# Group A's attention scores: one PSUM tile for each head instead of one for a pair of heads, and the sinks' exponentials in SBUF

## The chip, the cores and the metric

The kernel runs on one core of one Trainium2 chip. The metric is the device time of one execution in microseconds (us), from which the median over several runs is taken. The engines are named as in the profile: PE is the matrix engine (PEld is its loading of weights, which overlaps with matmuls), DVE is VectorE, ACT is ScalarE, POOL is GpSimd, and SP issues the DMAs. Each engine works through its own list of instructions in order and waits on semaphores for the others.

## The reference

One block of a streaming encoder on x of 1024 tokens by 1024 features: an input projection, two groups of attention heads side by side, an output projection with residual, and a feed-forward part. The change touches group A, eight heads that share two K/V heads, with a window of keys, a distance penalty and a learned sink for each head:

```python
n = rms_norm(h, norm1_g[layer])
proj = jnp.einsum('bsd,dp->bsp', n, w_in[layer])
qa, ka, va, qb, kb, vb = jnp.split(proj, split_at, axis=-1)
...
scores = jnp.einsum('bnqhgd,bnshd->bnhgqs', qc, kb).astype(jnp.float32) * (HEAD_DIM ** -0.5)
scores = scores - slopes[:, :, None, None] * dist
scores = jnp.where(valid[None, :, None, None, None, :], scores, NEG_INF)
m = jnp.maximum(jnp.max(scores, axis=-1, keepdims=True), sink)
p = jnp.exp(scores - m)
probs = (p / (jnp.sum(p, axis=-1, keepdims=True) + jnp.exp(sink - m))).astype(v.dtype)
out = jnp.einsum('bnhgqs,bnshd->bnqhd', probs, vb)
```

Group B is attention over nine chunks with a position bias and no sink. Both outputs are normalised and projected, and `h + squared-ReLU MLP` follows.

## The kernel before

Float32 operands are split into a high and a low part, so that one product takes two or three matmuls. The work runs in stages: the first projections, the attention of group A (about 42 to 184 us of the span), that of group B (to about 400 us), the output projection, and the two large feed-forward products.

Attention is cut into units. A `UnitA` is one pair of heads (`j`, 0 to 3; its two heads are `s` = 0 and 1) and two blocks of 128 query tokens (`i0` and `i0 + 1`; `b` = 0 and 1); there are 16. Tile names carry both, so `S_A0_4` holds the scores of pair 0 for blocks 4 and 5. The views shorten the names: `S_A0_4` stands in the order of instructions as `S_A_4` and a buffer number, in the trace as `S_A`. A unit has a first half, `score(0)` and `score(1)`, and a second half, two `turn`s and two `apply`s.

- `score(s)`: four matmuls write head `s`'s scores of both blocks into the PSUM tile `S` (line 129, called from `scores`). For each block DVE adds the bias and takes the row's negative maximum `nm` in one instruction (line 405, followed by a short read of the accumulator); ACT takes the exponentials and their sum `sm` (line 406). In `score(1)`, after both heads, ACT takes the two sinks' exponentials `es` (line 507, 128x2 each), DVE adds them to `sm` (line 508) and takes the reciprocal `rc` (line 509), and DVE and POOL scale the four blocks of probabilities `P` (line 512), two each.
- `turn(u)`: PE transposes blocks of `P` into the PSUM tile `pt` (line 132), ACT copies it to the high part of `T` (line 413) and DVE subtracts to get the low part (line 135).
- `apply(u)`: PE multiplies `T` with V into `av` (line 129); ACT copies one half of it to `yc` (line 548), DVE adds the other half into `Y` (line 549).

Before the change the tile `S` of a unit spans two PSUM banks: head 0's scores lie in the first, head 1's in the second, and `es` is written over the first four columns of head 0's. Two such tiles exist (`bufs=2`), and group B's tiles, of the same size, use the same two buffers:

```python
self.S = aps.tile([P, 2, 2, 2 * P], F32, tag="S", bufs=2, name=f"S_{self.name}")
...
es = self.S[:, 0, 0, :4]
```

PE's instructions keep the order in which the program is written (`pe` chains each matmul to the one before). While a unit's second half runs, the first half of the unit two further on is woven in (`interleave`, `look_ahead`, `LOOK_AHEAD = 2`), and `Filler` puts pieces of the next input projections between (`ip_qA`, `ip_kB` and so on; `A_FILL = 7` pieces for a unit). A projection ends with DVE scaling the accumulated bank into `ts_...` (lines 246 to 251), which frees the bank; the banks tagged `w` (three) are shared by projections and transposes. The order of instructions on DVE, ACT, POOL and SP is set by a scheduler when the kernel is built, from the data and buffer dependencies and its own estimates.

Of the kernel before, what the change touches and what calls it, by code (L numbers as in the profile page):

```python
# [8 lines left out]
F32 = mybir.dt.float32  # L9
# [6 lines left out]
P = 128  # L16
# [29 lines left out]
def kernel(  # L46
# [31 lines left out]
    small = ctx.enter_context(tc.tile_pool(name="small", bufs=4))  # L78
# [23 lines left out]
    nc.scalar.activation(warm, eps4, AF.Sqrt)  # L102


    small.tile([P, 120], F32, tag="pad", bufs=1, name="pad")

    last_load = [None]

# [19 lines left out]
    def matmul(*args, **kw):  # L128
        pe(nc.tensor.matmul(*args, **kw))  # L129
# [236 lines left out]
    aps = ap_.enter_context(tc.tile_pool(name="aps", bufs=1, space=PSUM, reuse_waits="tile"))  # L366
# [10 lines left out]
    def window(kind, i):  # L377

        nb = min(i, 1 if kind == "A" else 4) + 1
        return i - nb + 1, nb * P  # L380

    def scores(kind, i, Q, K, S):
        k0, n = window(kind, i)
        if n > 512:
            parts = [(S[:, 0, :320], 0, 320), (S[:, 1, :320], 320, 320)]
        else:
            w = max(n, 2 * P)
            parts = [(S[:, 0, :w], 0, w)]
        for hl in range(2):
            for dst, o, w in parts:  # L390
                matmul(
                    dst, Q[:, i * P : (i + 1) * P], K[hl][:, k0 * P + o : k0 * P + o + w],
                    start=hl == 0, stop=hl == 1,
                )

    def exponentials(kind, i, bias, init, S, pr, nm, sm):

        k0, n = window(kind, i)
        w = (2 if kind == "A" else 5) * P
        bs = bias[:, w - n : w]  # L400
        if n > 512:
            v = lambda a: a.rearrange("p (a b) -> p a b", a=2)
            nc.vector.tensor_tensor_reduce(v(pr[:, :n]), S[:, :, :320], v(bs), -1.0, init, ALU.add, ALU.min, nm)
        else:
            nc.vector.tensor_tensor_reduce(pr[:, :n], S[:, 0, :n], bs, -1.0, init, ALU.add, ALU.min, nm)  # L405
        nc.scalar.activation(pr[:, :n], pr[:, :n], AF.Exp, bias=nm, scale=-1.0, accum_out=sm)  # L406
        return k0, n, pr

    def stats(name):
        return [small.tile([P, 4], F32, tag=t, name=f"{t}_{name}") for t in ("nm", "sm", "rc")]  # L410
# [65 lines left out]
    class UnitA:  # L476
# [10 lines left out]
        def score(self, s):  # L487
            p, j = self.pair, self.pair.j
            if s == 0:
                self.nm, self.sm, self.rc = stats(self.name)  # L490
                self.S = aps.tile([P, 2, 2, 2 * P], F32, tag="S", bufs=2, name=f"S_{self.name}")
            pt = at.tile([P, 5 * P], F32, tag="P", bufs=6, name=f"P_{self.name}_{s}")
            h = 2 * j + s
            for b in range(2):
                scores("A", self.i0 + b, p.Q[s], p.K[j // 2 :: 2], self.S[:, s, b : b + 1])
            for b in range(2):
                c = slice(2 * s + b, 2 * s + b + 1)
                self.P[b, s] = exponentials(
                    "A", self.i0 + b, p.biases()[s], nsink[:, h : h + 1],
                    self.S[:, s, b : b + 1], pt[:, b * 2 * P : (b + 1) * 2 * P], self.nm[:, c], self.sm[:, c],  # L500
                )
            if s == 0:
                return
            es = self.S[:, 0, 0, :4]
            for s in range(2):
                c = slice(2 * s, 2 * s + 2)
                nc.scalar.activation(es[:, c], self.nm[:, c], AF.Exp, bias=psink[:, 2 * j + s : 2 * j + s + 1])
            nc.vector.tensor_tensor(self.sm, self.sm, es, ALU.add)
            nc.vector.reciprocal(self.rc, self.sm)
            for (b, s), (k0, n, q) in self.P.items():  # L510
                engine = nc.gpsimd if (b, s) in POOL_NORM else nc.vector
                engine.tensor_scalar(q[:, :n], q[:, :n], self.rc[:, 2 * s + b : 2 * s + b + 1], None, ALU.mult)
# [316 lines left out]
    X, F, S = {}, {}, {}  # L829
# [378 lines left out]
    g, p, n0 = order2[-GQ]  # L1208
    for q in (0, 2, 1, 3):
        for n in range(n0, n0 + GQ):  # L1210
            (uh, ul), (wh, wl) = ops2[n, p]
            c = slice(q * P, (q + 1) * P)
# [35 lines left out]
def build(arrays):  # L1248
    import concourse.bacc as _bacc

    nc = _bacc.Bacc("TRN2", target_bir_lowering=False, num_devices=1)
    args = [nc.dram_tensor(f"in_{n}_dram", arrays[n].shape, F32, kind="ExternalInput").ap() for n in _INS]
    args.append(nc.dram_tensor("out_0_dram", (SEQ, D), F32, kind="ExternalOutput").ap())
    with tile.TileContext(nc, schedule_with_timeline_sim=True) as tc:
        kernel(tc, *args)
    return nc
# [9 lines left out]
```

## Time and profile before

| what | value |
|---|---|
| median of 3 runs | 1073.88 us (1073.26 to 1074.16) |
| profiled execution, own time | 1074.59 us |
| its span, first to last instruction | 1072.5 us |
| mean granted TensorE clock | 0.996 |
| PE busy | 1050.7 us, 98% of the span |
| DVE, ACT, POOL busy | 706.3, 579.5, 416.7 us |

The spans of matmuls overlap: a matmul starts before the one ahead of it has ended, and its end is modelled, so a busy PE is not idle but need not be at its peak. What PE loses is read from its idle times and the granted clock. Some 22 us of the span are without a matmul, in the first projections, in group A's stage and at the very end.

### The profile page before, as it was taken

The numbers are of one execution on the slowest core, as the hardware profiler recorded it, in microseconds if no ns is written. First come the engines' busy times: TensorE is split into PE (matmuls) and PEld (weight loads), VectorE is DVE, ScalarE is ACT, GpSimd is POOL, SyncE is SP. The second block draws the span as 40 slices with busy tenths as digits, with TensorE's granted clock in tenths as the row PEclk, the third lists the DMA queues.
The fourth block names the chain that finished last, engine by engine and source line by source line (L and its number), as shares of the span: only waits on it lengthen the run. The fifth ranks groups of instructions, "written<-read, shape, count | busy, mean of one in ns | idle before, by whom it ended". The sixth has DMA issues, their size and how long they took to land.

```text
span 1072.5 us, 14369 instructions
## 1 busy us (share of the span) xinstructions
PE 1050.7 (98%) x5040; PEld 874.1 (82%) x5040; DVE 706.3 (66%) x1134; ACT 579.5 (54%) x994; POOL 416.7 (39%) x316
## 2 busy tenths in 40 slices
PE   7989999999999999999999999999999999999997
PEld 6877887888888888888888888888888888888885
DVE  4567778657667675696544434326889886778667
ACT  7666776656565465666544544554623333333346
POOL 1465766333361142405553464445015024024025
PEclk9999999999999999999999999999999999999999
DMA  9944626343457333133455344516998534532004
GB/s 328 261 114 115 171 89 173 101 111 112 134 191 282 129 108 137 79 98 118 181 172 177 140 135 158 190 65 235 317 403 302 182 126 161 178 119 96 1 1 157
DMA packets 90439, 170.17 MB, mean 159 GB/s; under 512 B 7808, under 2 KB 43520, under 8 KB 90368
## 3 DMA queue, kind: packets, MB, share of 16 engines
q1 hardware_dynamic: 90224, 169.25, 47.9%
q8 instruction: 40, 0.66, 0.2%
q14 instruction: 31, 0.25, 0.1%
q10 hardware_dynamic: 144, 0.00, 0.0%
HBM read 105.26 MB, written 45.09 MB: 140 GB/s over the span
## 4 chain that ended last, share of the span: by engine, by line
PE 86%; DVE 6%; issue 3%; DMA 2%; ACT 2%; SPq 1%; POOL 1%; DVEq 0%; ACTq 0%; POOLq 0%
PE f L129 27%; PE f_a L129 16%; PE f_c L129 8%; PE op_B L129 4%; PE f_b L129 4%; PE op_A L129 4%; PE ip_qB L129 4%; PE ip_kB L129 3%; PE ip_vB L129 3%; PE av_B L129 3%; PE pt_B L132 2%; PE S_B L129 2%; PE ip_qA L129 2%; PE S_A L129 1%; PE av_A L129 1%
## 5 line engine op out<-in xcount | busy, mean ns | idle before, releaser
L129 PE MATMUL f<-X,W 128*128 128x512 f32 x1344 | 305.9, 389 | 0.1
L129 PEld LDWEIGHTS f<-X,W 128*128 128x128 f32 x1344 | 252.0, 188 | 52.8 <-DVE X L135 0.5
L129 PE MATMUL f_a<-V,U 128*128 128x512 f32 x768 | 176.1, 389 | 0.0
L129 PEld LDWEIGHTS f_a<-V,U 128*128 128x128 f32 x768 | 144.1, 188 | 30.0
L135 POOL TENSOR_TENSOR U<-u,U 128x1024 fp32r<-128x1024 f32 x32 | 80.3, 2511 | 226.9 <-PE f_c L129 133.4
L135 POOL TENSOR_TENSOR W<-T,W 128x1024 fp32r<-128x1024 f32 x29 | 75.7, 2613 | 139.1 <-ACT W L934 139.1
L129 PE MATMUL f_c<-V,U 128*128 128x512 f32 x384 | 88.4, 389 | 0.0
L129 PEld LDWEIGHTS f_c<-V,U 128*128 128x128 f32 x384 | 72.1, 188 | 15.0
L934 ACT ACTIVATE V<-Z 128x1024 fp32r<-128x1024 f32 x32 | 33.9, 1060 | 90.6 <-PE f_a L129 44.6
L983 DVE TENSOR_TENSOR k<-f,k 128x1024 f32<-128x1024 f32 x24 | 29.3, 1221 | 61.9 <-PE f L129 61.9
L135 POOL TENSOR_TENSOR W<-w,W 128x1024 fp32r<-128x1024 f32 x23 | 57.3, 2492 | 32.2 <-ACT W L934 32.0
L934 ACT ACTIVATE V<-w 128x1024 fp32r<-128x1024 f32 x24 | 25.5, 1061 | 78.5 <-issue 34.2
L135 DVE TENSOR_TENSOR V<-w,V 128x1024 fp32r<-128x1024 f32 x24 | 47.2, 1972 | 27.4 <-ACT V L934 27.4
L934 ACT ACTIVATE U<-u 128x1024 fp32r<-128x1024 f32 x56 | 58.5, 1045 | 11.4 <-DMA ud<-k 7.8
L406 ACT ACTIVATE P_B<-P_B,nm_B 128x640 f32<-128x640 f32 (+2 forms) x64 | 44.4, 694 | 24.5 <-DVE nm_B L405 12.7
L977 ACT ACTIVATE k<-f 128x1024 f32<-128x1024 f32 x24 | 24.6, 1026 | 58.7 <-PE f L129 58.7
L129 PE MATMUL ip_kB<-nT,w_kB 128*128 128x512 f32 x192 | 51.5, 397 | 1.5 <-DVE T_A L135 0.8
L129 PE MATMUL op_A<-w_o,y 128*128 128x512 f32 x192 | 52.1, 397 | 0.5 <-DVE h L726 0.5
L129 PE MATMUL ip_vB<-nT,w_vB 128*128 128x512 f32 x192 | 51.9, 398 | 0.0
L934 ACT ACTIVATE W<-T 128x1024 fp32r<-128x1024 f32 x32 | 33.9, 1059 | 33.3 <-PE f L129 21.0
L129 PE MATMUL ip_qB<-nT,w_qB 128*128 128x512 f32 x192 | 51.5, 396 | 0.0
L129 PE MATMUL ip_qA<-nT,w_qA 128*128 128x512 f32 x192 | 51.3, 406 | 0.0
(212 smaller groups left out, 2033.2 us busy)
## 6 DMA issues: line engine op xcount, KB each, us to landing
w<-in_w_ff_dram SPq DMA_DIRECT2D x64, 512.0 KB, 4.7
u<-ud SPq DMA_DIRECT2D x56, 512.0 KB, 4.7
ud<-k SPq DMA_DIRECT2D x48, 512.0 KB, 3.2
KkB<-ts_kB SPq DMA_DIRECT2D x64, 128.0 KB, 2.3
yd<-y SPq DMA_DIRECT2D x14, 512.0 KB, 2.8
y<-yd SPq DMA_DIRECT2D x14, 512.0 KB, 7.1
xs<-in_xT_dram SPq DMA_DIRECT2D x16, 256.0 KB, 5.3
xr<-in_x_dram SPq DMA_DIRECT2D x8, 512.0 KB, 7.2
```

The source lines that it names most:

```text
L129: pe(nc.tensor.matmul(*args, **kw))
L132: pe(nc.tensor.transpose(*args))
L135: engine.tensor_tensor(lo, full, f(hi), ALU.subtract)
L406: nc.scalar.activation(pr[:, :n], pr[:, :n], AF.Exp, bias=nm, scale=-1.0, accum_out=sm)
L934: nc.scalar.activation(w[0], full, AF.Copy)
L977: nc.scalar.activation(kept[p], ps, AF.Copy)
L983: dve.tensor_tensor(v, ps, v, ALU.add)
```

## The change

Each head gets a PSUM tile `S` of its own, of the shape that group B uses, of which only the first bank is filled; still two buffers. The sinks' exponentials go to a small SBUF tile `es` with two buffers. A filler tile in the same SBUF pool is made smaller, so that later tiles keep their place.

```diff
-    small.tile([P, 120], F32, tag="pad", bufs=1, name="pad")
+    small.tile([P, 104], F32, tag="pad", bufs=1, name="pad")
...
             if s == 0:
                 self.nm, self.sm, self.rc = stats(self.name)
-                self.S = aps.tile([P, 2, 2, 2 * P], F32, tag="S", bufs=2, name=f"S_{self.name}")
+            S = aps.tile([P, 2, 512], F32, tag="S", bufs=2, name=f"S_{self.name}_{s}")
+            S = S[:, 0].rearrange("p (a b) -> p a b", a=2)
...
-                scores("A", self.i0 + b, p.Q[s], p.K[j // 2 :: 2], self.S[:, s, b : b + 1])
+                scores("A", self.i0 + b, p.Q[s], p.K[j // 2 :: 2], S[:, b : b + 1])
...
-                    self.S[:, s, b : b + 1], pt[:, b * 2 * P : (b + 1) * 2 * P], self.nm[:, c], self.sm[:, c],
+                    S[:, b : b + 1], pt[:, b * 2 * P : (b + 1) * 2 * P], self.nm[:, c], self.sm[:, c],
...
-            es = self.S[:, 0, 0, :4]
+            es = small.tile([P, 4], F32, tag="es", bufs=2, name=f"es_{self.name}")
```

PE's list has the same matmuls in the same order; its waits differ. The place shown is in the stretch near 57 us, where pair 0's unit of blocks 0 and 1 begins its `apply` (`av`) and head 1 of blocks 4 and 5 gets its scores (`S_A_4` before, `S_A_4_1` now). Before:

```order
L129 MATMUL av_A_0_723<-T_A_0_0_688,VA_175 128x256 [waits Activation_49]
L129 MATMUL av_A_0_723<-T_A_0_0_688,VA_175 128x256 [waits DVE_49]
L129 MATMUL S_A_4_707<-KA_171,QA_178 128x256 [waits DMAHW2_49,DMAHW0_49,DVE_49]
L129 MATMUL S_A_4_707<-KA_173,QA_178 128x256
L129 MATMUL S_A_4_707<-KA_171,QA_178 128x256
L129 MATMUL S_A_4_707<-KA_173,QA_178 128x256
```

Now:

```order
L129 MATMUL av_A_0_727<-T_A_0_0_692,VA_175 128x256 [waits Activation_49]
L129 MATMUL av_A_0_727<-T_A_0_0_692,VA_175 128x256 [waits DVE_49]
L129 MATMUL S_A_4_1_730<-KA_171,QA_178 128x256 [waits DMAHW2_49,DMAHW0_49]
L129 MATMUL S_A_4_1_730<-KA_173,QA_178 128x256
L129 MATMUL S_A_4_1_730<-KA_171,QA_178 128x256
L129 MATMUL S_A_4_1_730<-KA_173,QA_178 128x256
```

The wait for DVE ahead of head 1's scores is gone. It stands before each of the 16 units' head 1 before the change, and is left in one of them now (the first that takes a used buffer).

On DVE, the same place: the sinks' sum, reciprocal and scaling for blocks 2 and 3, the low part of the first transposes (`T_A_0_0`), and the maxima of blocks 4 and 5, head 0. Before:

```order
L508 TENSOR_TENSOR sm_A_2_629<-sm_A_2_629,S_A_2_631 128x4 [waits Activation_49]
L509 RECIPROCAL rc_A_2_630<-sm_A_2_629 128x4 [waits DVE_49]
L135 TENSOR_TENSOR T_A_0_0_688<-pt_A_0_0_687,T_A_0_0_688 128x256 [waits Activation_49]
L512 TENSOR_SCALAR P_A_2_0_632<-P_A_2_0_632,rc_A_2_630 128x256 [waits DVE_49]
L512 TENSOR_SCALAR P_A_2_1_661<-P_A_2_1_661,rc_A_2_630 128x256
L405 ISA P_A_4_0_708,nm_A_4_704<-S_A_4_707,b_A_318,nsink 128x256 [waits PE_49]
```

Now:

```order
L509 TENSOR_TENSOR sm_A_2_631<-sm_A_2_631,es_A_2_673 128x4 [waits Activation_49]
L510 RECIPROCAL rc_A_2_632<-sm_A_2_631 128x4 [waits DVE_49]
L513 TENSOR_SCALAR P_A_2_0_634<-P_A_2_0_634,rc_A_2_632 128x256 [waits DVE_49]
L513 TENSOR_SCALAR P_A_2_1_664<-P_A_2_1_664,rc_A_2_632 128x256
L135 TENSOR_TENSOR T_A_0_0_692<-pt_A_0_0_691,T_A_0_0_692 128x256 [waits Activation_49]
L405 ISA P_A_4_0_712,nm_A_4_708<-S_A_4_0_711,b_A_318,nsink 128x256 [waits PE_49]
```

`T_A_0_0`, for which `av` waits on PE, now stands behind the two scalings instead of ahead of them.

On ACT, the same place: the exponentials of head 1 of blocks 2 and 3, the two sinks' exponentials of that unit, and a weight copy of 128x1024 (`w_qA`). Before:

```order
L406 ACTIVATE P_A_2_0_632,sm_A_2_629<-P_A_2_0_632,nm_A_2_628 128x256 [waits DVE_49] x2
L252 ACTIVATE ts_qA_0_649<-ts_qA_0_649 128x512 [waits DMAHW4_49,DMAHW3_49,DMAHW5_49,DMAHW2_49,DMAHW6_49,DMAHW1_49,DMAHW7_49,DMAHW0_49,DVE_49]
L406 ACTIVATE P_A_2_1_661,sm_A_2_629<-P_A_2_1_661,nm_A_2_628 128x256 [waits DVE_49] x2
L507 ACTIVATE S_A_2_631<-nm_A_2_628,psink 128x2
L172 ACTIVATE w_qA_755<-st_qA_754 128x1024 [waits Pool_49]
L507 ACTIVATE S_A_2_631<-nm_A_2_628,psink 128x2 [waits Activation_49]
```

Now:

```order
L406 ACTIVATE P_A_2_0_634,sm_A_2_631<-P_A_2_0_634,nm_A_2_630 128x256 [waits DVE_49] x2
L508 ACTIVATE es_A_2_673<-nm_A_2_630,psink 128x2
L252 ACTIVATE ts_qA_0_651<-ts_qA_0_651 128x512 [waits DMAHW3_49,DMAHW4_49,DMAHW2_49,DMAHW5_49,DMAHW1_49,DMAHW6_49,DMAHW0_49,DMAHW7_49,DVE_49,Activation_49]
L406 ACTIVATE P_A_2_1_664,sm_A_2_631<-P_A_2_1_664,nm_A_2_630 128x256 [waits DVE_49] x2
L508 ACTIVATE es_A_2_673<-nm_A_2_630,psink 128x2
L172 ACTIVATE w_qA_761<-st_qA_760 128x1024 [waits Pool_49]
```

Head 0's sink now comes right behind head 0's exponentials, and head 1's stands ahead of the weight copy instead of behind it. The same is seen in the other units: the sinks come earlier on ACT, and on DVE the sum and the reciprocal stand ahead of the first addition into `Y` in 12 of them, as do POOL's two scalings ahead of its other work (`ts_...` and `w_...`) in several.

## Rows read from the trace of the kernel before

**Rows 1.** The page, part 1: busy us, share of the span, instructions.

```profile
PE 1050.7 (98%) x5040; PEld 874.1 (82%) x5040; DVE 706.3 (66%) x1134; ACT 579.5 (54%) x994; POOL 416.7 (39%) x316
```

**Rows 2.** Stretches: us, busy us (instructions) by engine, granted clock, DMA share, GB/s.

```profile
58.90:107.00 48.10, 44.95 (x238) 37.72 (x239) 34.32 (x99) 31.74 (x93) 27.82 (x30) 0.96 0.39 107
...
184.00:400.00 216.00, 214.34 (x1184) 181.37 (x1184) 149.19 (x376) 129.60 (x286) 80.35 (x95) 1.00 0.47 146
```

**Rows 3.** PE's and PEld's waits, 37 to 184 us: total, times, longest.

```profile
PE S_A L129 <- DVE nm_A L405: 3.3, 2, 1.9
PE pt_A L132 <- DVE ts_qA L249: 1.0, 1, 1.0
PE ip_kB L129 <- DVE T_A L135: 0.8, 1, 0.8
PE ip_kB L129 <- DVE ts_qA L249: 0.7, 1, 0.7
PE av_A L129 <- DVE T_A L135: 0.6, 1, 0.6
...
PEld S_A L129 <- DVE nm_A L405: 4.8, 5, 2.1
```

**Rows 4.** PE's timeline: start, us, instruction, [idle before and its releaser].

```profile
58.84 0.74 PE L129 MATMUL S_A<-KA,QA 128*128 128x256 f32 x4 [1.89 <-DVE nm_A L405]
...
77.30 0.75 PE L129 MATMUL S_A<-KA,QqA 128*128 128x256 f32 x4 [1.43 <-DVE nm_A L405]
...
90.77 0.66 PE L132 MATMUL pt_A<-ident,P_A 128*128 128x128 f32 x4 [1.03 <-DVE ts_qA L249]
...
99.93 1.67 PE L129 MATMUL ip_kB<-nT,w_kB 128*128 128x512 f32 x6 [0.68 <-DVE ts_qA L249]
```

**Rows 5.** DVE's timeline ahead of the first of these waits.

```profile
55.78 0.16 DVE L508 TENSOR_TENSOR sm_A<-sm_A,S_A 128x4 f32<-128x4 f32 x1 [2.17 <-ACT S_A L507]
...
56.43 1.55 DVE L512 TENSOR_SCALAR P_A<-P_A,rc_A 128x256 f32<-128x256 f32 x2
...
58.71 0.08 DVE L405 DVE_READ_ACCUMULATOR2_ANT nm_A<- 128x1 f32 x1
```

**Rows 6.** ACT's timeline at the same place.

```profile
54.55 1.04 ACT L172 ACTIVATE w_qA<-st_qA 128x1024 fp32r<-128x1024 f32 x1
...
55.50 0.25 ACT L507 ACTIVATE S_A<-nm_A,psink 128x2 f32<-128x2 f32 x1
```

**Rows 7.** Stretches around the first long wait, columns as in Rows 2.

```profile
57.00:58.80 1.80, 0.00 (x0) 0.00 (x0) 1.80 (x7) 0.38 (x1) 1.80 (x4) 1.00 0.22 48
...
60.40:63.70 3.30, 3.30 (x9) 2.60 (x8) 1.66 (x8) 2.46 (x9) 1.49 (x2) 0.50 0.57 159
...
63.80:75.90 12.10, 12.07 (x71) 10.25 (x69) 9.24 (x21) 7.22 (x19) 5.68 (x6) 1.00 0.32 75
```

**Rows 8.** Lines 507 and 144, small activations: ns min/median/max, first and last.

```profile
L507 ACT ACTIVATE S_A<-nm_A,psink x32: 242/248/267, 47.4 to 166.9; 128x2 f32<-128x2 f32 x32
...
L144 ACT ACTIVATE u_n<-ss,eps x10: 283/296/298, 22.4 to 455.0; 128x1 f32<-128x1 f32 x8, 128x4 f32<-128x4 f32 x2
```

**Rows 9.** DVE's and ACT's timeline ahead of the wait at 99.93 us.

```profile
97.45 0.42 DVE L549 TENSOR_TENSOR Y<-av_A,yc 64x256 f32<-64x256 f32 x1 [2.41 <-ACT yc L548]
...
99.20 0.68 DVE L249 SCALAR_TENSOR_TENSOR ts_qA<-ip_qA,R 128x512 f32<-128x512 f32 x1
...
95.24 1.06 ACT L172 ACTIVATE w_qB<-st_qB 128x1024 fp32r<-128x1024 f32 x1
```

**Rows 10.** DVE's and PE's timeline: a read ends, the same head's next scores.

```profile
44.17 0.09 DVE L405 DVE_READ_ACCUMULATOR2_ANT nm_A<- 128x1 f32 x1
...
47.52 0.72 PE L129 MATMUL S_A<-KA,QA 128*128 128x256 f32 x4
```

**Rows 11.** POOL's timeline: a weight's low part, then two scalings.

```profile
55.67 2.89 POOL L135 TENSOR_TENSOR w_qA<-st_qA,w_qA 128x256 fp32r<-128x256 f32 x4 [0.83 <-ACT w_qA L172]
58.54 1.82 POOL L512 TENSOR_SCALAR P_A<-P_A,rc_A 128x256 f32<-128x256 f32 x2
```


## The prediction

> **What bounds the kernel now.** I read the page first: PE is busy for 1050.7 us of a span of 1072.5 [rows 1], so the end moves only by what PE idles or runs slowly. Next the table of stretches. Group A's stage is the one with holes in the middle of the run: from 58.9 to 107 us PE is busy for 44.95 of 48.10 us at a granted clock of 0.96, while in group B, with DVE about as full, it is busy for 214.34 of 216.00 [rows 2]. Then the list of waits in that stage. The largest is "S_A waits for nm_A": head 1's scores wait for line 405 on DVE, 3.3 us as PE sees it (2 times), 4.8 us as the weight loads see it (5 times); the other four entries come to 3.1 us [rows 3]. The timeline puts the two long ones at 58.84 and 77.30 us [rows 4].
>
> What does this wait need? At 58.84 DVE has just read out the maximum of blocks 4 and 5 of head 0 (the read at 58.71 takes 0.08 us) [rows 5], and PE, which starts at once, writes head 1's scores of the same two blocks. They lie in another bank, and no number passes between the two. PE waits because both heads' scores are one tile. And DVE is late with that maximum since it stood still for 2.17 us for the sinks [rows 5]: on ACT the second sink came at 55.50, behind a weight copy of 1.04 us [rows 6].
>
> The clock tells of a second loss. PE is idle from 57.0 to 58.8. From 60.4 to 63.7 the granted clock is 0.50, that is 1.2 GHz in place of 2.4: PE is busy throughout, but starts 9 matmuls in 3.30 us, where the next stretch at 1.00 has 71 in 12.10 [rows 7]. That is the only fall from 58.9 to 107 us: 3.4 us at half speed out of 48.1 are what a mean of 0.96 leaves room for [rows 2]. The idle time of 1.43 us ahead of 77.30 [rows 4] brought none. So the first, longer one is the likely cause, and it is the wait that the change removes.
>
> **The change, part by part.**
>
> *The wait of head 1.* The list of PE loses it in 15 of 16 units. Price: 3.3 us by PE's idle times, 4.8 by those of the weight loads [rows 3]. Ends of matmuls are modelled and overlap with the next start, so PE's figure is too low by a little at each of the five waits, and the other is an upper end. I take 4.3.
>
> *The clock.* 3.4 us at half speed cost 1.7 us, and nothing if it falls all the same. I take 1.7, since the idle time before it should go almost wholly.
>
> *The sinks come earlier.* They no longer wait for head 1's part of the tile, so ACT takes head 0's sink right behind its exponentials, and the second one before the weight copy. In the unit of rows 5 and 6 that is 1.04 us earlier, and DVE's sum, reciprocal and scalings with it. At the wait at 99.93 us PE wants a bank that DVE frees by line 249 at 99.20 plus 0.68; ahead of that, DVE idled 2.41 us until an addition into Y, behind which the sum stood, and ACT spent 1.06 us on a weight copy amid the unit's exponentials [rows 9]. Now the copy comes after them and the sum before the addition, so the 0.68 us of waiting there [rows 4] should vanish. At 90.77 us (1.03 us [rows 4]) the same line 249 has moved ahead of one addition of 0.42 us and follows a sum that waits for one sink less (0.25 us): 0.7 of the 1.03 go. Of the wait of `ip_kB` for a transpose, 0.8 us [rows 3], I count 0.1. Bounds: nothing, and all three, 1.0 + 0.7 + 0.8 = 2.5 us. I take 1.5.
>
> *The sinks go to SBUF.* No row of before has this exponential with an SBUF target. The nearest is line 144, a small activation into SBUF of 296 ns against 248 for line 507 into PSUM [rows 8]: 0.05 us more, 32 times 1.6 us of ACT, which has room in group A (31.74 us busy of 48.10 [rows 2]). It touches the end only where DVE waits for the second sink: in every one of 16 units that would be 0.8 us, the upper bound; the lower is no difference. I take 0.1, two such places. The Trainium skill (ScalarE: Activation LUTs, Step-by-step: what each stage is for) speaks against the edit here: it says that ScalarE reaches PSUM faster than SBUF. The two rows agree in sign, though their functions differ (square root and exponential), and by either the sum moves by 0.8 us at most.
>
> *What is late next.* PE comes to its next waits some 2 to 4 us earlier. (a) `T_A_0_0` now stands behind two scalings, which took 1.55 us in the old place, with POOL at work beside them [rows 5]. DVE's sum can start about 1.0 us sooner, so `av` waits some 0.3 us longer than before; at worst 0.6 (1.55 less the 1.0). (b) POOL does its two scalings before the weight copy's low part, which began at 55.67 [rows 11]. The reciprocal is there at about 55.0, the two scalings take 1.82 us, a piece 2.89 / 4 = 0.72 [rows 11]: the first piece is ready at about 57.6. PE fell idle at 58.84 - 1.89 = 56.95; with 0.3 us of (a), the four scores (0.74) and five projection matmuls (1.67 / 6 = 0.28 each, ends overlapping) [rows 4] it needs the piece at about 59. Covered by a us or more; if scalings beside DVE's take longer, some 0.5 us. (c) DVE is busy for 34.32 of 48.10 us [rows 2], and the removed waits gave it time to catch up; it may end a transpose or a projection's scaling late in a few units. Bounds: nothing, and all that head 1 gave, 4.3 us. I take 0.8 of (c), which is one wait of the kind seen at 90 or 154 us, and 0.3 + 0.1 for (a) and (b).
>
> *Two buffers for single heads.* A head's scores now wait until the same head's tile of the unit before has been read. The smallest distance I find in the trace is at the beginning: the tile read at 44.17 plus 0.09, the same head's next scores at 47.52 [rows 10], so 3.3 us of room. Nothing is charged. After group A, PE has next to no waits [rows 2], so what is gained stays gained.
>
> **Sum**, against the profiled execution of 1074.59 us: 1074.6 - 4.3 - 1.7 - 1.5 + 0.1 + (0.3 + 0.1 + 0.8) = 1068.4. The median of the runs shown lies 0.7 us below the profiled one, so 1067.7.
>
> **The rivals.**
>
> 1. *The waits go, the clock falls or DVE takes part of it back.* DVE's late maxima were a sign that it was behind; PE would then stand at `av` (waiting for T) or at a bank in place of the scores. For it: the other four entries of the waits all name DVE [rows 3]. Against: DVE's idle times of 2.17 and 2.41 us show that it waits as well. If half of the 4.3 + 1.5 comes back and the clock falls, 1.7 + 2.9 less the 1.2 already counted: 1067.7 + 3.4 = 1071.1. The Trainium skill (TensorE: Matmul & The Clock Gate, A second HAM failure mode: psum-queue depth-cycling) describes a kernel in which small idle times between groups of matmuls were enough to make the clock swing. In this trace the 1.43 us ahead of 77.30 us were not enough [rows 4]; that counts against it.
>
> 2. *The change does nothing that can be measured.* Head 1's wait would be only the first of several on one chain through DVE (maximum, scaling, transpose's low part), and PE would wait as long a little later: 4.3, 1.7 and 1.5 all come back, and 1073.5 to 1073.9 remains. Against it: only 5 of the 16 units show that wait at all [rows 3], so DVE keeps up in general.
>
> 3. *Slower: the ring of two heads.* If DVE's reads of one unit fall more than 3.3 us behind, the next unit's scores of that head wait for them, where before a whole unit lay between. From 3.3 us of further lateness on, each us costs PE one us in each unit concerned. With 5 us of it, 1.7 more than the room, in four units: 4 x 1.7 = 6.8 us on top of the forecast, 1074.5, and with one more fall of the clock 1076.2. Against it: no such lateness is in the trace, and the sinks, which held DVE up ahead of 58.84 [rows 5], come earlier.
>
> **How the numbers follow.** The forecast gets 0.64, rival 1 0.20, rival 2 0.11, rival 3 0.05. About 0.2% (2.1 us) is what a measurement of this kernel can tell from no change, so the bound for "faster" is 1071.7. The forecast lies wholly on that side, of rival 1 most: 0.64 + 0.17 = 0.81 faster. Same: 0.03 + 0.11 + 0.01 = 0.15. Slower 0.04. The upper bounds of all gains with nothing given back make 1074.6 - 4.8 - 1.7 - 2.5 - 0.7 = 1064.9; a range of 1065.3 to 1071.9 leaves out the end of that, rivals 2 and 3.
>
> **What the profile after would show.** Right: no entry "S_A waits for nm_A" for PE, or one below 0.3 us; PE's granted clock at 1.00 from 58.9 to 107 us; in the stage of group A some 3 us less idle time for PE; the sum at line 509 without DVE idle times of 2 us ahead of it. Wrong: a new entry of more than 2 us for `av_A` waiting for T_A, or for the projections waiting for line 249; a clock of 0.50 somewhere in the stage; scores of either head waiting for nm_A of the unit before; or a first small-exponential duration far above 0.3 us. The prediction would also be wrong if the stage ended 6 us earlier and a later transfer of weights, started from it, held PE up in group B.

## The result, and the profile after

The changed kernel takes 1067.07 us, median of 6 runs (1066.10 to 1068.89). The kernel before, run beside it, takes 1073.91 us (6 runs, 1073.26 to 1075.31). The ratio on record is 0.9944, 95% interval 0.9933 to 0.9954; ratios here are not quotients of the two medians (that would be 0.9936), so the two differ a little throughout. Two more comparisons of the same pair, further below, gave 0.9951 and 0.9948. By these ratios the change gains 5.3 to 6.0 us; the medians of the three comparisons lie 6.8, 5.2 and 4.5 us apart. That is over twice the 0.2% that can be told from no change; the forecast was 1067.7.

The profiled execution took 1068.89 us, its span is 1067.0. Its page has these sums of busy time, to be held against [rows 1]:

```profile
PE 1049.3 (98%) x5040; PEld 874.3 (82%) x5040; DVE 710.5 (67%) x1134; ACT 578.5 (54%) x994; POOL 413.1 (39%) x316
```

No engine's work has changed by more than 4.2 us. The work is the same; what went is time in which PE stood idle or ran at half its clock. The waits of PE in group A's stage, from 37 to 184 us (engine, operation and line, what was waited for, us in total, times, longest), answer to [rows 3]:

```profile
PE av_A L129 <- DVE Y L550: 1.3, 1, 1.3
PE pt_A L132 <- DVE ts_vB L246: 0.6, 1, 0.6
PE av_A L129 <- DVE T_A L135: 0.6, 1, 0.6
PE ip_kB L129 <- DVE ts_qA L249: 0.4, 1, 0.4
PE ip_kB L129 <- DVE T_A L135: 0.2, 1, 0.2
```

"S_A waits for nm_A" is gone. The first two lines are new: one wait of 1.3 us for an addition into Y, and one of 0.6 us for a projection's bank. The timeline of PE, cut to the rows with a wait in brackets, shows where they stand (it answers to [rows 4]):

```profile
93.11 1.67 PE L129 MATMUL ip_kB<-nT,w_kB 128*128 128x512 f32 x6 [0.43 <-DVE ts_qA L249]
138.19 0.65 PE L132 MATMUL pt_A<-ident,P_A 128*128 128x128 f32 x4 [0.64 <-DVE ts_vB L246]
147.43 0.96 PE L129 MATMUL ip_kB<-nT,w_kB 128*128 128x512 f32 x3 [0.25 <-DVE T_A L135]
172.82 0.36 PE L129 MATMUL av_A<-T_A,VA 128*128 128x256 f32 x1 [1.29 <-DVE Y L550]
173.80 1.01 PE L129 MATMUL av_A<-T_A,VA 128*128 128x256 f32 x3 [0.62 <-DVE T_A L135]
```

From 58.9 to 92 us PE now does not wait at all. The table of stretches (length; busy us of each engine with the number of instructions that run in it, those across its edges included; PE's granted clock; share of the DMA engines; GB/s) says it again, beside [rows 2], and shows a second place:

```profile
58.90:107.00 48.10, 47.55 (x266) 40.26 (x265) 37.35 (x109) 34.10 (x99) 32.32 (x35) 1.00 0.48 135
168.00:184.00 16.00, 14.09 (x67) 11.53 (x66) 8.81 (x28) 8.11 (x20) 6.89 (x8) 0.89 0.53 149
184.00:400.00 216.00, 214.80 (x1188) 182.30 (x1187) 148.56 (x371) 129.82 (x285) 79.56 (x94) 1.00 0.48 151
173.70:177.10 3.40, 3.30 (x10) 2.92 (x11) 1.52 (x6) 0.08 (x1) 1.18 (x2) 0.52 0.41 103
```

From 58.9 to 107 us the clock is at 1.00 and 266 matmuls run where 238 did. But from 168 to 184 us, where group A ends and group B begins, it is 0.89: behind the two waits at 172.82 and 173.80 lie 3.4 us at about half clock, in which 10 matmuls run. Before the change this stretch ran at 1.00:

```profile
168.00:184.00 16.00, 15.38 (x82) 12.84 (x81) 13.69 (x37) 9.96 (x24) 9.40 (x12) 1.00 0.79 209
```

So the fall of the clock [rows 7] did not vanish, it moved. Because PE's matmuls keep their order, one and the same matmul can be found in both traces, and its start tells how much had been gained by then. Before, the end of group A reads:

```profile
178.85 0.34 PE L129 MATMUL av_A<-T_A,VA 128*128 128x256 f32 x1
179.81 0.62 PE L129 MATMUL av_A<-T_A,VA 128*128 128x256 f32 x3 [0.62 <-DVE T_A L135]
...
182.01 0.62 PE L129 MATMUL av_A<-T_A,VA 128*128 128x512 f32 x2
```

and after:

```profile
177.55 0.63 PE L129 MATMUL av_A<-T_A,VA 128*128 128x512 f32 x2
```

PE was ready for the first of these `av` at 172.82 - 1.29 = 171.53, against 178.85: 7.3 us gained by then. (The stage itself began 0.4 us later than before, its first scores at 42.46 against 42.09, so within the stage it is 7.7.) PE started that `av` 178.85 - 172.82 = 6.0 us earlier, and the last ones 182.01 - 177.55 = 4.5 us earlier: the new wait took 1.3 back and the halved clock some 1.5. At the end of the span it is 1072.5 - 1067.0 = 5.5 us. The 1 us more did not come bit by bit: it came in group B near 320 us, where PE before the change waits twice:

```profile
319.85 0.71 PE L129 MATMUL av_B<-padL,VvB 128*128 128x256 f32 x2 [0.23 <-ACT padL L413]
...
322.32 0.44 PE L132 MATMUL pt_B<-ident,P_B 128*128 128x128 f32 x2 [0.25 <-DVE VvB L135]
```

ACT's `padL` stands right behind its copy of an output weight (`w_o`, at 318.48), which had waited 2.56 us for a transfer. After the change the same copy waits 1.20 us, PE has no wait at these two matmuls, and its lead over the kernel before grows there from 4.4 us (317.84 against 313.40) to 5.6 (322.32 against 316.74). Why that transfer is waited for less is not followed here.

What is the new wait? It begins on the DMA queue. The rows that matter, from the timeline of all engines, in order of time:

```profile
162.34 0.52 SPq L439 DMA_DIRECT2D b_B<-in_relb_dram  x1
...
167.83 0.14 POOL L440 MEMSET b_B<- 64x64 f32 x1 [1.82 <-DMA b_B<-in_relb_dram]
168.03 0.15 POOL L441 MEMSET b_B<- 64x64 f32 x1
168.26 1.29 POOL L468 TENSOR_TENSOR sqA<-sqA,y 128x512 f32<-128x512 f32 x1
169.58 1.06 ACT L172 ACTIVATE w_vB<-st_vB 128x1024 fp32r<-128x1024 f32 x1 [2.21 <-POOL sqA L468]
170.55 0.71 ACT L406 ACTIVATE P_B<-P_B,nm_B 128x512 f32<-128x512 f32 x1
171.37 0.38 ACT L549 ACTIVATE yc<-av_A 64x256 f32<-64x256 f32 x1
172.26 0.42 DVE L550 TENSOR_TENSOR Y<-av_A,yc 64x256 f32<-64x256 f32 x1
```

A position bias of group B is issued at 162.34 and lands at 167.8, 5.5 us later. POOL stands still for it for 1.82 us, since it writes two masked corners into that tile (lines 440, 441). Its sum of squares `sqA` comes behind; ACT's weight copy waits 2.21 us for that sum; behind the copy stand an exponential and `yc`, behind `yc` DVE's addition into Y, and behind that PE's `av`. Before the change the same chain is in the trace, with a landing of 3.2 us and room to spare:

```profile
169.28 0.54 SPq L439 DMA_DIRECT2D b_B<-in_relb_dram  x1
...
172.47 0.14 POOL L440 MEMSET b_B<- 64x64 f32 x1 [2.62 <-DMA b_B<-in_relb_dram]
174.02 1.29 POOL L468 TENSOR_TENSOR sqA<-sqA,y 128x512 f32<-128x512 f32 x1
...
175.34 1.06 ACT L172 ACTIVATE w_vB<-st_vB 128x1024 fp32r<-128x1024 f32 x1 [0.49 <-POOL sqA L468]
```

The copy waited for 0.49 us there and PE not at all.

### The profile page after: what moved, and what is told of

It is laid out like the page before. It is cut to its first block, busy times and chain, and to the rows that moved or that the text cites. A ratio compares the mean times of both kernels' runs of the same rounds, so it can differ in the third digit from the quotient of the medians.

```text
span 1067.0 us, 14388 instructions
## 1 busy us (share of the span) xinstructions
PE 1049.3 (98%) x5040; PEld 874.3 (82%) x5040; DVE 710.5 (67%) x1134; ACT 578.5 (54%) x994; POOL 413.1 (39%) x316
## 4 chain that ended last, share of the span: by engine, by line
PE 91%; DVE 4%; DMA 2%; issue 1%; ACT 1%; SPq 1%; POOL 0%; DVEq 0%; ACTq 0%; POOLq 0%
PE f L129 27%; PE f_a L129 16%; PE f_c L129 8%; PE op_B L129 4%; PE f_b L129 4%; PE op_A L129 4%; PE ip_qB L129 4%; PE ip_kB L129 4%; PE ip_qA L129 4%; PE ip_vB L129 3%; PE av_B L129 3%; PE S_B L129 2%; PE pt_B L132 2%; PE S_A L129 1%; PE av_A L129 1%
## 5 line engine op out<-in xcount | busy, mean ns | idle before, releaser
L935 ACT ACTIVATE V<-w 128x1024 fp32r<-128x1024 f32 x24 | 25.4, 1060 | 81.1 <-issue 34.2
L135 DVE TENSOR_TENSOR V<-w,V 128x1024 fp32r<-128x1024 f32 x24 | 49.9, 2081 | 28.0 <-ACT V L935 27.1
L135 DVE TENSOR_TENSOR V<-Z,V 128x1024 fp32r<-128x1024 f32 x32 | 46.2, 1445 | 9.4 <-ACT V L935 5.9
```

The costliest lines, as they stand in the source:

```text
L135: engine.tensor_tensor(lo, full, f(hi), ALU.subtract)
L935: nc.scalar.activation(w[0], full, AF.Copy)
```

## The experiments

The theory: head 1's scores waited for head 0's maxima only because both lay in one tile; with two tiles that wait goes, and the earlier sinks, which is the second half of the change, shorten what is left on DVE. Rivals: the second half alone does it, since DVE's lateness came from the sinks; or SBUF as the place for the sinks brings the gain. Three comparisons were made, each with its own runs of the kernel before: there 1071.96 us in the first (17 runs, 1071.38 to 1074.32), 1073.03 in the second (15 runs, 1071.16 to 1074.86), 1072.85 in the third (10 runs, 1071.59 to 1075.12).

**The second half alone: shared tile, sinks in SBUF.** Against the kernel before:

```diff
-    small.tile([P, 120], F32, tag="pad", bufs=1, name="pad")
+    small.tile([P, 104], F32, tag="pad", bufs=1, name="pad")
...
-            es = self.S[:, 0, 0, :4]
+            es = small.tile([P, 4], F32, tag="es", bufs=2, name=f"es_{self.name}")
```

> One half alone: the sinks' exponentials in SBUF, but both heads' scores in one tile as before. Every engine's order is that of the changed kernel (two rows apart on DVE, one on POOL), and the wait of head 1 on DVE is back in all 16 units. My theory (wait, clock and early sinks each count): the early sinks bring DVE's maxima forward by about 1 us at the two long waits, so they shrink from 2.1 and 1.6 us to about 1.0 and 0.7, too short for the clock to fall: 1068.5 to 1070. If the shared tile is all (rival: the sinks do nothing): about 1073.5. If the early sinks are all (rival: the wait is harmless once DVE is in time): 1067, with no entry of S_A waiting for nm_A over 0.3 us.

Measured: 1071.05 us (11 runs, 1070.22 to 1072.11), ratio 0.9989 (0.9980 to 0.9998). That is worse than the 1068.5 to 1070 expected. The waits of PE in its trace, 37 to 184 us:

```profile
PE av_A L129 <- ACT P_B L406: 2.4, 1, 2.4
PE pt_A L132 <- DVE ts_vB L246: 0.6, 1, 0.6
PE av_A L129 <- DVE T_A L135: 0.6, 1, 0.6
PE S_A L129 <- DVE nm_A L405: 0.6, 2, 0.4
```

Two things follow. The wait of head 1, with the tile still shared, has shrunk from 3.3 us to 0.6 by the sinks alone: most of it was DVE being late, not the sharing as such. And most of the gain was lost again at the change of groups, where `av` waits 2.4 us through the same chain (POOL's fill stands for 5.68 us until the bias lands at 168.5) and the clock is 0.89 from 168 to 184 us.

**The first half alone: two tiles, sinks in PSUM.** The sinks' exponentials lie over head 1's scores, so they come as late as before. Against the changed kernel:

```diff
-    small.tile([P, 104], F32, tag="pad", bufs=1, name="pad")
+    small.tile([P, 120], F32, tag="pad", bufs=1, name="pad")
...
-            es = small.tile([P, 4], F32, tag="es", bufs=2, name=f"es_{self.name}")
+            es = S[:, 0, :4]
```

> The other half alone: a tile for each head, but the sinks' exponentials in PSUM, over head 1's scores. ACT, DVE, POOL and SP keep the order of the kernel before (the sinks late), and head 1 no longer waits. My theory: the 4.3 us of waits and the 1.7 us of clock go, the 1.5 us of the early sinks do not come: 1068 to 1069.5, PE now waiting at 90 and 99 us for line 249 as before, about 1.0 and 0.7 us. If the early sinks are all: 1073.5. If the tiles are all: 1067.

Measured: 1069.30 us (6 runs, 1068.10 to 1069.72), ratio 0.9969 (0.9958 to 0.9981), as expected. The wait of head 1 is gone; those for the projections are not:

```profile
85.49 0.66 PE L132 MATMUL pt_A<-ident,P_A 128*128 128x128 f32 x4 [1.04 <-DVE ts_qA L249]
94.96 1.65 PE L129 MATMUL ip_kB<-nT,w_kB 128*128 128x512 f32 x6 [1.02 <-DVE ts_qA L249]
148.91 0.97 PE L129 MATMUL ip_kB<-nT,w_kB 128*128 128x512 f32 x3 [1.06 <-DVE T_A L135]
```

In the changed kernel the same three are nothing, 0.43 and 0.25. That is what the early sinks add: 3.1 - 0.7 = 2.4 us, less the changed kernel's 0.64 at 138.19, which this variant does not have. In this variant the clock stays up at the change of groups, where the waits are 0.34 and 0.62 us (POOL's fills are in it as well; the table below comes back to this).

**Two tiles, sinks in PSUM over head 0's scores.** Head 0's tile has been read when head 1's exponentials run, so the sinks come early without SBUF. Against the changed kernel:

```diff
+            if s == 0:
+                self.S0 = S
...
-            es = small.tile([P, 4], F32, tag="es", bufs=2, name=f"es_{self.name}")
+            es = self.S0[:, 0, :4]
```

> A tile for each head, the sinks' exponentials in PSUM, over head 0's scores. The order on POOL and SP is that of the changed kernel, on DVE and ACT it differs in some 15 to 30 rows; head 0's tile is held until the sum is read. This tells whether SBUF as such matters or only that the sinks don't wait for head 1's part of a shared tile. My theory: the place is worth nothing on PE's path (0.05 us for each activation): 1067 to 1068, line 508 near 250 ns in place of what the changed kernel shows. If PSUM is faster enough to count: below 1066.5. If the ring of two tiles binds once a tile is held longer: scores waiting for line 509, above 1069.

Measured: 1067.39 us (5 runs, 1065.67 to 1069.54), ratio 0.9960 (0.9947 to 0.9974). Its interval overlaps with that of the changed kernel in all three comparisons, and its waits ahead of 160 us are those of the changed kernel (0.37 at 93.05, 0.25 at 146.58 us) without the one at 138.19. One sink takes 245 ns here and 280 in the changed kernel. SBUF as the place is worth nothing that shows; what counts is that the sinks wait for no later scores.

**The chain at the change of groups taken away.** The bias of group B gets its masked corners where the input is laid out, and POOL's two fills are left out, so POOL no longer waits for that transfer. Against the changed kernel:

```diff
-                    nc.gpsimd.memset(b[:HD, 5 * P - HD :], NEG)
-                    nc.gpsimd.memset(b[HD:, :HD], NEG)
...
+    band[:, :64, 576:] = NEG
+    band[:, 64:, :64] = NEG
```

> The changed kernel with group B's masked corners (NEG in two 64x64 corners of each bias tile) written into the input's layout, so that POOL's two memsets for each head are left out and POOL no longer waits for the bias transfer. In the changed kernel's profile POOL waits 1.8 us for it at 167.8, ACT 2.2 us for POOL behind that, and PE idles 1.3 + 0.6 us at 172.8 and 173.8, after which the clock is 0.50 for 3.4 us. My theory (a chain from the transfer through POOL and ACT to PE, then the clock): these go, up to 3 us in executions that had them, so 1065 to 1066.3, with a smaller scatter than the 1066.1 to 1068.9 of the changed kernel. Rival (PE waits there for DVE's or ACT's own work): 1067 and the same wait at 172.

Measured: 1066.76 us (5 runs, 1065.90 to 1067.05), ratio 0.9947 (0.9934 to 0.9959). The median is above the 1065 to 1066.3 expected; the scatter is smaller, as expected (1.2 us against 2.8 for the changed kernel). The two waits at the change of groups, from its timeline of PE:

```profile
172.09 0.36 PE L129 MATMUL av_A<-T_A,VA 128*128 128x256 f32 x1 [0.45 <-ACT T_A L413]
173.07 0.62 PE L129 MATMUL av_A<-T_A,VA 128*128 128x256 f32 x3 [0.62 <-DVE T_A L135]
```

And the stretch around them, from its table of stretches:

```profile
168.00:184.00 16.00, 14.88 (x77) 11.91 (x75) 11.99 (x33) 7.77 (x21) 4.79 (x7) 1.00 0.53 149
```

The wait of 1.29 us has become one of 0.45, and the clock stays at 1.00. So POOL's fills, which wait for the bias, are what let it reach PE. They did so only where the bias landed late, as the traces with the fills in place show (us; the last two rows are later profiles of the changed kernel, from the comparisons below):

| kernel | bias issued | POOL's fill starts | between | PE's wait at that `av` | clock, 168 to 184 |
|---|---|---|---|---|---|
| before | 169.28 | 172.47 | 3.2 | none | 1.00 |
| two tiles, late sinks | 163.65 | 166.94 | 3.3 | 0.34 | 1.00 |
| two tiles, sinks over head 0's scores | 161.42 | 166.15 | 4.7 | 0.47 | 1.00 |
| shared tile, sinks in SBUF | 162.93 | 168.51 | 5.6 | 2.40 | 0.89 |
| the changed kernel | 162.34 | 167.83 | 5.5 | 1.29 | 0.89 |
| the same, second profile | 161.36 | 167.15 | 5.8 | 1.47 | 0.89 |
| the same, third profile | 162.08 | 168.37 | 6.3 | 2.40 | 0.89 |

**Both halves apart, without that chain.** Since the first two variants differ at the change of groups, they were run again with the corners in the input: the kernel before, its two tiles alone, its sinks in SBUF alone (the diffs are those above, combined), and the changed kernel as it is.

> The kernel before with group B's masked corners in the input (POOL's two memsets left out), the base for the next two. In the kernel before PE has no wait at 172 us, so this should be the same as before: ratio 0.999 to 1.001. If the memsets cost something by themselves: 1 to 3 us faster.

> That base with a tile for each head and the late sinks (over head 1's scores). The order on DVE and ACT is the base's but for a few rows. From the start-to-start losses on PE between 38 and 110 us (10.6 us before, 6.0 with tiles only, 4.8 with the sinks only, 3.8 with both): 3 to 4.6 us faster than the base, the larger figure in executions of the base whose clock falls. If the shared tile were not the cause of the wait: as the base.

> That base with the sinks' exponentials in SBUF and one tile for both heads; every engine's order is that of the run with the mask in the input, two rows of DVE apart. The run with the sinks only was 1071.05 us, but had 2.4 us of idle time and a fall of the clock at 175 us, behind POOL's memset. My theory now: the two halves remove the same wait, either by not waiting or by having DVE ready, so that without the stall at 175 us this is within 1.5 us of both halves together, 5 to 6 us faster than the base. Rival: the early sinks themselves bring the stall at 175 us, by another way than the memsets: about 1071 again, and PE idle there for over 2 us.

> The changed kernel once more, beside the following three on one chip. PE idles at the end of group A's stage (172 us) in its profile, while the run with the mask in the input does not. If that wait and the fall of the clock behind it come in a part of the executions only, the times scatter over 2 to 3 us (clock 0.997 in the long ones, 0.998 to 0.999 in the short ones) around a ratio of 0.994 to 0.996. If the two kernels differ in every execution: all long ones.

| variant | us (runs) | range | ratio (95% interval) |
|---|---|---|---|
| corners in the input alone | 1073.91 (11) | 1071.96 to 1074.96 | 1.0002 (0.9993 to 1.0011) |
| with two tiles | 1068.73 (5) | 1067.96 to 1068.99 | 0.9957 (0.9944 to 0.9969) |
| with sinks in SBUF | 1068.56 (5) | 1068.00 to 1068.81 | 0.9956 (0.9943 to 0.9970) |
| the changed kernel | 1067.85 (5) | 1066.09 to 1069.11 | 0.9951 (0.9938 to 0.9963) |

The corners alone bring nothing, as expected. With them, either half gains about 4.4 us against the kernel before of that comparison, and 5.2 and 5.4 against the corners alone (3 to 4.6 and 5 to 6 were expected), where the two together gain 5.2 (1071.96 - 1066.76, in the first comparison) or 5.8 (1072.85 - 1067.04, in the third). The halves overlap: one lets PE pass the late maximum, the other makes it come in time. The kernel with the corners alone also says something of the clock. From its timeline of PE:

```profile
57.50 0.74 PE L129 MATMUL S_A<-KA,QA 128*128 128x256 f32 x4 [1.34 <-DVE nm_A L405]
74.36 0.74 PE L129 MATMUL S_A<-KA,QqA 128*128 128x256 f32 x4 [1.41 <-DVE nm_A L405]
```

and from its table of stretches:

```profile
58.90:107.00 48.10, 44.63 (x249) 37.69 (x248) 35.85 (x103) 33.10 (x94) 28.36 (x31) 1.00 0.42 117
```

The waits of head 1 are there, and the clock is at 1.00. The runs hint at how often: its 11 times fall into a group of 1071.96 to 1072.48 us with a mean clock of 0.998 to 0.999 (5 runs) and one of 1073.91 to 1074.96 (6 runs, five of them at 0.997). Read so, a fall would come in about half of this kernel's executions and cost some 2 us where it comes. No trace of this kernel shows one, and the run of 1074.00 us has a mean clock of 0.999, so this is a reading of run times and not shown.

**The changed kernel and the one with the corners, side by side.**

> The changed kernel once more, beside the version with the corners of group B's bias in the input. Theory: a wait of 1.2 to 1.5 us for Y near 172 us and, in most executions, a stretch at clock 0.50 behind it; 0.994 to 0.9955 of before. Rival (the corners change nothing): the same.

> The changed kernel with the corners of group B's bias in the input and without POOL's two fills. Theory: the wait near 172 us is below 0.6 us, the clock stays at 1.00 there, and the median lies 0.5 to 1.7 us below that of the changed kernel on the same chip. Rival: the idle time at the change of groups is covered by the clock staying up in most executions anyway, and the two medians differ by less than 0.4 us.

Measured: 1068.32 us (6 runs, 1066.47 to 1069.54), ratio 0.9948 (0.9934 to 0.9962), and 1067.04 us (6 runs, 1066.18 to 1067.52), ratio 0.9938 (0.9925 to 0.9950). The changed kernel's profiled execution waits longer than the 1.2 to 1.5 us expected, as its timeline of PE shows:

```profile
173.59 0.35 PE L129 MATMUL av_A<-T_A,VA 128*128 128x256 f32 x1 [2.40 <-DVE Y L550]
```

With the corners in the input the same matmul waits for 0.43 us:

```profile
173.12 0.35 PE L129 MATMUL av_A<-T_A,VA 128*128 128x256 f32 x1 [0.43 <-ACT T_A L413]
```

The median is 1.28 us lower, inside the 0.5 to 1.7 expected, and the longest of its 11 runs in two comparisons is 1067.52 us, where 11 of the changed kernel's 17 runs lie above that. The intervals of the two ratios overlap, so the size of this gain is known only roughly; its cause is in the traces. This version has the lowest medians here (1066.76 and 1067.04 us).

## Why the prediction was right

*The wait of head 1 (-4.3).* It went wholly, as forecast, and the clock from 58.9 to 107 us is 1.00. The first of the two long waits was worth more than its idle time of 1.89 us. Two scores in a row, before the change,

```profile
54.34 0.72 PE L129 MATMUL S_A<-KA,QA 128*128 128x256 f32 x4
```

with the next at 58.84 [rows 4], and after it:

```profile
54.35 0.72 PE L129 MATMUL S_A<-KA,QA 128*128 128x256 f32 x4
...
56.53 0.64 PE L129 MATMUL S_A<-KA,QA 128*128 128x256 f32 x4
```

They lay 4.50 us apart and now lie 2.18 apart, 2.3 us less. What was off is the reason given for the term's size. The sharing of the tile was one of two conditions: with the tile still shared, early sinks alone cut the wait from 3.3 to 0.6 us. So the terms for the wait and for the sinks are not the gains of the two edits; either edit takes most of the first term, and only what DVE does later for the projections belongs to the sinks alone.

*The clock (-1.7).* The price of one fall was right: between the `av` at 172.82 and that at 177.55 some 1.5 us of the lead were lost. But the term counted a fall as if every execution of the kernel before had it, and the changed kernel has one of its own in all three of its profiles. How often either comes can only be guessed from the runs. Of the changed kernel's 17, 9 show a mean clock of 0.996 or 0.997 (median 1068.8 us) and 8 show 0.998 or 0.999 (median 1066.6). Of the 42 of the kernel before in the three comparisons, it is 14 (median 1074.3) and 28 (median 1072.0). The mean clock is no sure sign of a fall, since each profile also has a low clock at its end, after PE's last matmul, where it costs nothing, and for 2.3 to 5.5 us. The last profile above, with the corners in the input, has a mean of 0.997 and a clock of 1.00 from 37 to 1060 us; this stretch, in which no matmul runs, is its low one (columns as in the tables of stretches):

```profile
1060.40:1065.70 5.30, 0.00 (x0) 0.00 (x0) 1.51 (x6) 0.73 (x2) 0.00 (x0) 0.50 0.54 199
```

So how the two falls balance on the medians is not shown. The execution from which the sum started had the fall, and so had the profiled one after; for these two the sum gave 1068.4 and the run took 1068.89 us.

*The sinks earlier (-1.5).* The wait at 90.77 us went wholly (0.7 of 1.03 counted), that at 99.93 went from 0.68 to 0.43, not to nothing, and that of `ip_kB` for a transpose from 0.8 to 0.25 (0.1 counted). Together 1.03 + 0.25 + 0.57 = 1.85 us. On DVE the sum is still held up by the sinks, but more briefly. The timeline of DVE after, with the read of the maximum for which head 1 used to wait:

```profile
54.40 0.18 DVE L509 TENSOR_TENSOR sm_A<-sm_A,es_A 128x4 f32<-128x4 f32 x1 [1.11 <-ACT es_A L508]
...
56.76 0.09 DVE L405 DVE_READ_ACCUMULATOR2_ANT nm_A<- 128x1 f32 x1
...
97.62 0.16 DVE L509 TENSOR_TENSOR sm_A<-sm_A,es_A 128x4 f32<-128x4 f32 x1 [0.94 <-ACT es_A L508]
```

The first sum waits 1.11 us, where it was 2.17, and the maximum is read at 56.76 in place of 58.71 [rows 5]; at the other place 0.94 us remain of 2.41 [rows 9].

*The sinks to SBUF (+0.1).* One sink takes 280 ns now against 248 [rows 8] (the row is of line 508's 32 instructions; min, median, max):

```profile
L508 ACT ACTIVATE es_A<-nm_A,psink x32: 278/280/286, 46.3 to 159.3; 128x2 f32<-128x2 f32 x32
```

32 ns more, where 0.05 us was reckoned from line 144. The rule of the Trainium skill cited in the prediction (ScalarE: Activation LUTs, Step-by-step: what each stage is for), that ScalarE reaches PSUM sooner than SBUF, agrees with this, now for one and the same function; in time it did not matter, as the variant with the sinks over head 0's scores shows.

*What is late next (+1.2).* This is the step that was mis-sized. `T_A_0_0` (a) costs PE nothing: the sum starts 55.78 - 54.40 = 1.4 us earlier, not 1.0, and the maxima that follow are early as well. POOL's weight piece (b) starts at 56.85, and with 2.85 us for four the first is done at about 57.6, as reckoned; PE does not wait for it. Of (c), 0.64 us came, the wait at 138.19 for a projection's bank. DVE scales that projection at 137.46, and the sinks' sum (at 134.98, after a wait of 0.86 us) and two scalings of `P` now stand ahead of it; before the change those scalings came behind it (143.89 against 143.29). The large wait of 1.29 us came at 172.82, from a transfer through POOL and ACT, with a fall of the clock behind it: 0.64 + 1.3 + 1.5 = 3.4 us in an execution with the fall, against 1.2 charged.

*Why the time came out right even so.* Among the signs that would make the forecast wrong stood "a clock of 0.50 somewhere in the stage", which appeared, and a new entry of more than 2 us for `av_A` waiting for T_A; what appeared was one of 1.29 us (2.40 in the third profile) for `Y`. That the time came out right in spite of both is in part luck. The gain up to that place is 7.3 us with the 0.64 and the 0.4 of later start already taken off, so 8.3 where 4.3 + 1.7 + 1.5 - 0.1 = 7.4 was reckoned; and the 1 us that came in group B was not in the sum at all ("what is gained stays gained"). These 1.9 us make up most of the 2.2 by which the charge was too small. The step from the execution to the median, 0.7 us, was 1.8 in the runs after, since the profiled one was the slowest of its six.

Rival 1 had the shape of what happened at 172.82, with DVE as the cause; the cause was the landing of a DMA. The Trainium skill (TensorE: Matmul & The Clock Gate, A second HAM failure mode: psum-queue depth-cycling) tells of a kernel whose small idle times between groups of matmuls come often enough to make the clock swing. Here the clock fell behind two idle times of 1.29 and 0.62 us in a row, and not behind single ones of 1.34 and 1.41 us in the kernel with the corners alone.

*The ring of two heads.* No wait for an older tile appears for `S_A`; the room was enough. Rival 3 is out, and rival 2 too.

## What to carry to other kernels

A wait that names data nobody needs (a maximum of the other half of a tile) can be taken away at both ends: split the tile, or find out why the data come late; either may give most of the gain, and the two gains don't add up. When a stage gets some us shorter, look at the next place where a transfer's landing is passed on through several engines' lists: here 7 us less used up its slack. And before a fall of the clock is booked as a gain, look at the times of several runs: one profile shows whether it happened that time, not how often it does, and a run's mean clock takes in stretches that cost nothing.

## What was not expected of the hardware

After a short idle time of PE the clock was halved for some us in five traces here, and not in others. Idle times of 1.89 us (ahead of 58.84, before), of 1.29, 1.47 and 2.40 us (the changed kernel's three profiles) and of 2.40 us (shared tile, sinks in SBUF), the last four each followed by 0.62 us more one matmul later, were followed by 3.4 us at 0.50 within a few us; idle times of 1.34, 1.41 and 1.43 us, alone, were not. No trace shows the same idle time once with and once without a fall. That the changed kernel and the kernel before have the fall in a part of their executions only is read from the spread of their run times and mean clocks, and not shown.

The landing of the same 320 KB bias took 3.2 us in the trace before and 5.5 in the one after, with the DMA engines busy for 0.93 of the first stretch and 0.91 of the second; why it took longer stays open.
